# Tile shapes on TensorE: a full-height low key part, transposes in a queue with the value matmuls, and sample scores side by side

## The chip, the cores and the metric

The kernel runs on one core of a Trainium2 chip. The metric is the device time of one execution, in microseconds (us). The engines are TensorE (PE, its weight loads shown apart as PEld), VectorE (DVE), ScalarE (ACT), GpSimd (POOL) and SyncE (SP), which issues most of the loads and stores.

## The reference

Shortened. One layer of a hybrid decoder, for a prompt of 512 tokens and for 8 samples of 4 tokens each that have a past of 2048 positions in a paged cache. The width is 1024.

```python
h = rmsnorm(x, w['g_mix'])
(q, kc_new, vc_new, ks_new, vs_new, kw_new, vw_new, g_nsa, xm, vm, om, i_pre, f_pre) = split_cols(h @ w['w_in'])
...
k_cmp = compress(kc_all, *w['cmp_k'])
v_cmp = compress(vc_all, *w['cmp_v'])
...
o_nsa = nsa_attend(q, k_cmp, v_cmp, ks_all, vs_all, kw_all, vw_all, gates, offset, w_pre)
...
hm, C, n, m = mlstm_chunked(qm, km, vm, i_pre + w['b_i'], f_pre + w['b_f'], C0, n0, m0)
...
x = x + jnp.concatenate([o_nsa, hm], axis=-1) @ w['w_out']
x = x + CrossAttn(rmsnorm(x, w['g_xa']), mem_k, mem_v)
h = rmsnorm(x, w['g_ffn'])
x = x + (jax.nn.silu(h @ w['w_gate']) * (h @ w['w_up'])) @ w['w_down']
y = rmsnorm(x, w['g_final'])
```

`nsa_attend` has 8 query heads over 2 key/value heads of width 64 and sums three softmax branches with gates: compressed blocks, the 16 best blocks of 64 keys, and a window of 512. For the prompt the selected and the windowed branch are plain causal attention over the up to 512 keys before a query; `br` below counts these two. All is float32, and a position's bias is its distance times a slope of the head.

## The kernel before

The 512 prompt tokens and the 32 sample tokens stand together as T = 544 columns, in two halves of 272. A dense matmul in float32 is made of three (`mm3`, L214 to L216): both operands are split into a high and a low part, and high by high, high by low and low by high are summed in one PSUM bank (`bd`, `xa`, `xc`).

A unit of prompt attention is (j, i, br): j of 4 heads in a group, i of 4 blocks of 128 queries, br of 2 branches, 32 units in all, and in each unit v runs over the two key/value heads. A unit goes through three steps:

- `score` (L566 to L591). For each v, L580 multiplies the 128 rows of Q2 (its high part in 64 rows and its low part in the other 64) by KK (the high part of the keys, standing twice, in both halves of the rows), and L581 adds the 64 rows with the high part of the queries times KL, the low part of the keys, which stands only in the rows of its own v. So L580 uses all 128 rows of the array and L581 uses 64. Then DVE adds the bias and finds the extreme (L585), ACT takes the exponential with a sum (L587), DVE the reciprocal (L588), and POOL scales by it and by the gate (L589).
- `turned` (L593 to L601). PE transposes the i + 1 blocks of 128 keys of each v by a matmul with the identity (L599, into one of two `tp` banks), and ACT copies them to SBUF (L601).
- `value` (L603 to L614). For each key block and v, L609 multiplies by 64 columns of values, so that it fills 64 of the array's 128 columns; v = 0 and v = 1 stand in different columns.

The generator (L616 to L625) emits the score of unit n, then the values of unit n - 2, then the transposes of unit n - 1. `weave` (L288) mixes it with the dense matmuls of the projections that follow; when those are used up, the rest of prompt attention is drained alone. The Tile framework then sets the final order on each engine, so matmuls that are emitted together may be taken apart; `tc.issue_after(x)` makes what is emitted inside it, on the same engine, stand behind x.

Sample attention (`sample`, L1375 to L1664) works on two groups g of four samples. Keys come from window buffers and by indirect loads that POOL issues (`gather`, L536), are transposed by PE in fours (`four_t`, L1474) and copied into one of four buffers `kt` (`keys`). The scores of a chunk of 512 keys are four matmuls, one for each sample of the group, each on 32 of the array's columns:

```python
for q, b in enumerate(bs):
    nc.tensor.matmul(S[32 * q:32 * q + 32], Qn[:, b], kts[q], start=True, stop=True)
```

This form stands at L1512 (window), at L1553 (compressed keys, 127 of them) and at L1604 (selected keys, four chunks for each group). Behind it DVE adds a mask and finds the extreme (L1605). The values follow at L1645 in the same 32-column form. This stage is woven with the second part of the compression.

Two more places: mLSTM's gate (L771) multiplies `nsel` by `M2`, 36 rows high; and at the end `to_rows` (L2466 to L2501) transposes the output tiles back to rows, of which the last has only the 32 sample tokens.

Of the kernel before, what the change touches and what calls it, by code (L numbers as in the profile page):

```python
# [16 lines left out]
T = 544  # L17
# [3 lines left out]
EPS = 1e-6  # L21
# [15 lines left out]
def body(tc, I, O, stage=99, dbg=None):  # L37
    nc = tc.nc
    with ExitStack() as top:
# [335 lines left out]
        KL = nn.tile([128, 2, 512], R32, name="KL")  # L375
        bd = nn.tile([128, 512], F32, name="bd")

        def prep_k():
# [8 lines left out]
            for br in range(2):  # L387
                c0 = 256 + 256 * br
                p = bank(ptp)
                for i in range(4):  # L390
                    nc.tensor.transpose(p[:, 128 * i:128 * i + 128], kvn[:, i, c0:c0 + 128], ident)
                for v in range(2):
                    a, b = slice(64 * v, 64 * v + 64), slice(64 - 64 * v, 128 - 64 * v)
                    nc.scalar.activation(KK[a, br, v], p[a], AF.Copy)
                    nc.vector.tensor_tensor(KL[a, br], p[a], KK[a, br, v], op=OP.subtract)
                    nc.gpsimd.tensor_copy(KK[b, br, v], KK[a, br, v])
                p = bank(ptp)
                nc.tensor.transpose(p[:, :32], kvs[:, c0:c0 + 128], ident[:32, :32])
                nc.vector.tensor_copy(kTs[:, br], p[:, :32])
                yield 2  # L400
# [165 lines left out]
        def nsa():  # L566
# [3 lines left out]
            def score(j, i, br):  # L570
# [5 lines left out]
                for v in range(2):  # L576
                    h = 4 * v + j
                    a = slice(64 * v, 64 * v + 64)
                    S = bank((psp, ppo)[v])
                    nc.tensor.matmul(S[:, :n], Q2[:, h, 128 * i:128 * i + 128], KK[:, br, v, :n], start=True, stop=False)  # L580
                    nc.tensor.matmul(S[:, :n], Q2[a, h, 128 * i:128 * i + 128], KL[a, br, :n], start=False, stop=True)  # L581
# [11 lines left out]
            def turned(j, i, br):  # L593
                n = 128 * i + 128
                for v in range(2):
                    sb = soft.pop((j, i, br, v))
                    p = bank(ptp)
                    for k in range(i + 1):
                        nc.tensor.transpose(p[:, 128 * k:128 * k + 128], sb[:, 128 * k:128 * k + 128], ident)  # L599
                    PT[j, i, br, v] = wp.tile([128, 512], F32, name="PT", bufs=4)  # L600
                    nc.scalar.activation(PT[j, i, br, v][:, :n], p[:, :n], AF.Copy)  # L601
# [123 lines left out]
        def mlstm():  # L725
# [5 lines left out]
            nsel = mq.tile([36, 4, 128], R32, name="nsel")  # L731
            M2 = mq.tile([36, 512], R32, name="M2")
# [11 lines left out]
            nc.vector.tensor_copy(nsel, zer[:36, 0:4, None].to_broadcast([36, 4, 128]))  # L744
            nc.vector.tensor_copy(M2, zer[:36, 0:1].to_broadcast([36, 512]))
# [628 lines left out]
        def sample():  # L1374
# [114 lines left out]
            for g in range(2):  # L1489
# [21 lines left out]
                for q, b in enumerate(bs):  # L1511
                    nc.tensor.matmul(S[32 * q:32 * q + 32], Qn[:, b], kts[q], start=True, stop=True)  # L1512
# [32 lines left out]
            for g in range(2):  # L1545
# [6 lines left out]
                for q, b in enumerate(bs):  # L1552
                    nc.tensor.matmul(pc[32 * q:32 * q + 32, 0:127], Qn[:, b], kcT[:, b, 0:127], start=True, stop=True)  # L1553
# [47 lines left out]
                for c in range(4):  # L1601
                    S = bank(psp)
                    for q, b in enumerate(bs):
                        nc.tensor.matmul(S[32 * q:32 * q + 32], Qn[:, b], kts[q], start=True, stop=True)  # L1604
# [860 lines left out]
        def to_rows(j, hf, p):  # L2465
# [10 lines left out]
            for q, i in enumerate(tiles):  # L2476
                m = tok[i][1]
                if i > 1:
                    nc.vector.tensor_tensor(yt[i][:m, cj], pt_[:m, 128 * q:128 * q + 128], yc[:m, 1, cj], op=OP.mult)
# [4 lines left out]
            for q, i in enumerate(tiles):  # L2484
                t0, m = tok[i]
                nc.tensor.matmul(pr[:m, q:q + 1], acct[:, t0:t0 + m], ones_d[:, 0:1], start=True, stop=True)
            r = rn[:, c0:c0 + n]
            if hf == 1:
                nc.vector.memset(r, 1.0)
            for q0, q1, m in (((0, 3, 128),) if hf == 0 else ((0, 1, 128), (1, 2, 32))):  # L2490
                nc.vector.tensor_scalar(r[:m, q0:q1], pr[:m, q0:q1], EPS, None, op0=OP.add)
            nc.gpsimd.tensor_tensor(r, r, mhalf[:, :n], op=OP.pow)
            for q, i in enumerate(tiles):
                t0, m = tok[i]
                y = yt[i]
                if q == 1:
                    nc.scalar.activation(y[:m], y[:m], AF.Copy, scale=r[:m, 1:2])
                else:
                    nc.vector.tensor_scalar(y[:m], y[:m], r[:m, q:q + 1], None, op0=OP.mult)
                dst = O[Y_P][0, t0:t0 + m] if t0 < 512 else O[Y_S].rearrange("b t d -> (b t) d")  # L2500
                nc.sync.dma_start(dst, y[:m])  # L2501
# [31 lines left out]
```

## Time and profile before

| what | us |
|---|---|
| median of three runs | 1302.64 |
| lowest, highest of them | 1298.22, 1302.9 |
| the profiled execution | 1297.18 |
| its span (first to last instruction) | 1295.2 |

The profile is that of one execution. In it a record's length holds its way through the array, and records overlap, so what a matmul costs PE is the time from its start to the start of the next. The stages, by the trace: projections to 110 us, prompt attention to 277.6, mLSTM and the first compression to 490.8, sample attention to 655.6, output mix and cross attention to 909, the gated feed-forward part to 1259, and the end.

### The profile page before, as it was taken

How to read it: one execution, taken by the hardware profiler on the slowest of the kernel's cores; microseconds unless marked ns; L12 is line 12 of the kernel's file. 1: busy time of each engine (PE TensorE's matmuls, PEld its weight loads, DVE VectorE, ACT ScalarE, POOL GpSimd, SP SyncE). 2: the span in 40 equal slices, each digit the busy share in tenths (PEclk: the TensorE clock that was granted, in tenths of full speed). 3: DMA queues.
4: the chain of work that ended last, by engine and by line, in shares of the span. 5: the costliest groups of instructions: out<-in, count | busy, mean ns of one | idle time of the engine just before them, and what ended most of it. 6: DMA issues, size and time to landing. Idle time of an engine off the chain costs nothing.

```text
span 1295.2 us, 25054 instructions
## 1 busy us (share of the span) xinstructions
PE 1231.2 (95%) x9388; PEld 1087.6 (84%) x9388; DVE 869.1 (67%) x1951; ACT 643.3 (50%) x1494; POOL 580.0 (45%) x692
## 2 busy tenths in 40 slices
PE   7999999999999789999999998999989999999996
PEld 5998777748987577766689988679979999999996
DVE  6246464366978978666665485743898888877874
ACT  4234545475646644456554333432555465465452
POOL 1003233257756765553334110014687377387443
PEclk8998999989999889999999999999989999999998
DMA  6424131023125353455678459942022332332311
GB/s 199 122 51 99 44 136 50 1 67 124 48 83 172 112 201 124 148 174 173 213 198 164 130 152 255 303 152 66 2 66 76 121 99 86 116 101 91 129 51 70
DMA packets 141772, 154.34 MB, mean 119 GB/s; under 512 B 17449, under 2 KB 123689, under 8 KB 141394
## 3 DMA queue, kind: packets, MB, share of 16 engines
q1 hardware_dynamic: 131922, 119.17, 30.8%
q0 software_dynamic: 9728, 33.56, 7.9%
q8 instruction: 74, 1.21, 0.4%
q14 instruction: 48, 0.39, 0.1%
HBM read 141.67 MB, written 13.12 MB: 120 GB/s over the span
## 4 chain that ended last, share of the span: by engine, by line
PE 71%; DVE 12%; DMA 5%; issue 4%; POOL 3%; ACT 2%; SPq 1%; POOLq 0%; DVEq 0%; ACTq 0%
PE xa L2208 7%; PE xc L2208 7%; PE bd L214 6%; PE bd L216 6%; PE bd L215 6%; PE bd L2208 5%; PE tp L2208 5%; PE xa L214 2%; PE tp L599 2%; PE xa L216 2%; PE xa L215 2%; PE sp L1604 1%; PE xc L215 1%; PE xc L214 1%; PE xc L216 1%
## 5 line engine op out<-in xcount | busy, mean ns | idle before, releaser
L210 POOL TENSOR_TENSOR al<-fraw,ah 128x512 fp32r<-128x512 f32 (+1 forms) x104 | 127.2, 1224 | 153.4 <-ACT ah L209 124.8
L209 ACT ACTIVATE whi<-wraw 128x1024 fp32r<-128x1024 f32 (+3 forms) x78 | 67.0, 900 | 64.2 <-DMA wraw<-in_w_xv 28.7
L210 DVE TENSOR_TENSOR wlo<-wraw,whi 128x1024 fp32r<-128x1024 f32 (+3 forms) x78 | 79.5, 1046 | 28.7 <-ACT whi L209 28.5
L209 ACT ACTIVATE ah<-fraw 128x512 fp32r<-128x512 f32 (+1 forms) x112 | 66.0, 594 | 41.5 <-PE xc L2208 11.8
L216 PE MATMUL bd<-w1h,xl 128*128 128x256 f32 x256 | 78.4, 307 | 5.1 <-DVE xl L210 2.9
L589 POOL TENSOR_SCALAR sb<-sb,rs,gat 128x128 f32<-128x128 f32 (+3 forms) x64 | 43.2, 678 | 86.8 <-DVE rs L588 73.3
L214 PE MATMUL bd<-w1h,xh 128*128 128x256 f32 x256 | 78.4, 306 | 0.3 <-ACT xh L209 0.3
L215 PE MATMUL bd<-w1l,xh 128*128 128x256 f32 x256 | 76.0, 297 | 0.0
L216 PEld LDWEIGHTS bd<-w1h,xl 128*128 128x128 f32 x256 | 52.2, 204 | 11.5 <-DVE xl L210 3.7
L214 PEld LDWEIGHTS bd<-w1h,xh 128*128 128x128 f32 x256 | 52.2, 204 | 7.6 <-issue 4.3
L209 ACT ACTIVATE xh<-xf 128x512 fp32r<-128x512 f32 x64 | 40.0, 629 | 33.3 <-DVE xf L1149 13.1
L1152 POOL TENSOR_TENSOR sf<-xf 128x256 f32<-128x256 f32 x48 | 35.5, 740 | 46.9 <-DVE sl L210 38.7
L209 ACT ACTIVATE ah<-sp 128x512 fp32r<-128x512 f32 (+1 forms) x64 | 35.6, 557 | 40.8 <-DVE sp L2148 19.2
L214 PE MATMUL bd<-hhi,whi 128*128 128x272 f32 x176 | 54.1, 308 | 0.2 <-ACT whi L209 0.2
L1149 DVE STREAM_TRANSPOSE xf<-cgat 128x512 f32<-128x512 f32 x64 | 44.9, 702 | 13.8 <-POOL sf L1152 13.4
L215 PE MATMUL bd<-hlo,whi 128*128 128x272 f32 x176 | 53.5, 304 | 0.0
L215 PEld LDWEIGHTS bd<-w1l,xh 128*128 128x128 f32 x256 | 52.2, 204 | 1.0 <-issue 0.7
L216 PE MATMUL bd<-hhi,wlo 128*128 128x272 f32 x176 | 53.0, 301 | 0.0
L601 ACT ACTIVATE PT<-tp 128x128 f32<-128x128 f32 (+3 forms) x64 | 27.7, 436 | 50.7 <-PE tp L599 50.2
L209 ACT ACTIVATE ah<-po 128x512 fp32r<-128x512 f32 (+1 forms) x64 | 35.7, 558 | 29.0 <-PE xa L2208 21.6
L585 DVE CUSTOM_DVE_ANT_0 sb<-po,BM 128x128 f32<-128x128 f32 (+3 forms) x32 | 15.7, 491 | 48.6 <-PE po L581 27.2
L216 PE MATMUL bd<-hh,wlo 128*128 128x272 f32 x160 | 46.9, 293 | 0.0
(997 smaller groups left out, 4985.7 us busy)
## 6 DMA issues: line engine op xcount, KB each, us to landing
fraw<-in_w_gate SPq DMA_DIRECT2D x11, 1024.0 KB
fraw<-in_w_up SPq DMA_DIRECT2D x11, 1024.0 KB
fraw<-in_w_down SPq DMA_DIRECT2D x24, 384.0 KB
mkv<-in_cache_mem_k SPq DMA_DIRECT2D x64, 128.0 KB
mkv<-in_cache_mem_v SPq DMA_DIRECT2D x16, 512.0 KB
wraw<-in_w_in SPq DMA_DIRECT2D x8, 512.0 KB
wraw<-in_w_xq SPq DMA_DIRECT2D x4, 1024.0 KB
wraw<-in_w_xk SPq DMA_DIRECT2D x4, 1024.0 KB
```

The source lines that it names most:

```text
L209: nc.scalar.activation(hi, src, AF.Copy)
L210: (eng or nc.gpsimd).tensor_tensor(lo, src, hi, op=OP.subtract)
L214: nc.tensor.matmul(out, ah, bh, start=first, stop=False, **kw)
L215: nc.tensor.matmul(out, ah, bl, start=False, stop=False, **kw)
L216: nc.tensor.matmul(out, al, bh, start=False, stop=last, **kw)
L585: nc.vector.tensor_tensor_reduce(sb[:, :n], S[:, :n], BM[v][:, 384 - 128 * i:512], 1.0, BIG, op0=OP.add, op1=OP.min, accum_out=mn)
L589: (nc.vector, nc.gpsimd)[1].tensor_scalar(sb[:, :n], sb[:, :n], rs, gat[:, i, 3 * h + 1 + br:3 * h + 2 + br], op0=OP.mult, op1=OP.mult)
L599: nc.tensor.transpose(p[:, 128 * k:128 * k + 128], sb[:, 128 * k:128 * k + 128], ident)
L601: nc.scalar.activation(PT[j, i, br, v][:, :n], p[:, :n], AF.Copy)
L1149: nc.vector.transpose(xf.rearrange("p a (q i) -> p q a i", q=4), gs[0].rearrange("p (q t a i) -> p t q a i", q=4, t=4, a=4)[:, t])
L1152: (nc.gpsimd if (1,1,1,1,1,0,1,0)[4 * kv + t] else nc.vector).tensor_tensor(sf, xf[:, :, 0:128:2], xf[:, :, 1:128:2], op=OP.add)
L2208: nc.tensor.matmul(p[:, :HALF], w[a][:, k], x[b_][:, k], start=first and k == 0 and i == 0, stop=last and k == n - 1 and i == 2, skip_grou ...
```

## The change

- KL is kept apart for each v and in full height: four more copies on POOL put it into the other 64 rows too, and L581 multiplies all 128 rows. The product gains the queries' low part times the keys' low part.
- `turned` takes one v. The transposes of v = 1 come first, and the value matmuls of unit n - 2 and the transposes of v = 0 are queued behind them on PE.
- `nsel` and `M2` get 68 rows instead of 36, the new ones zero.
- `quad` issues the four score matmuls of a chunk of sample keys, the fourth sample's first and the other three queued behind it. It is used at the three places named above.
- `to_rows` transposes 128 tokens for the last tile too (those from T - 128 on), whose sample tokens then stand in the partitions 96 to 127; its sums of squares likewise, and one `tensor_scalar` takes the place of a `memset` and two.

```diff
--- before.py
+++ after.py
@@ -372,7 +372,7 @@
-        KL = nn.tile([128, 2, 512], R32, name="KL")
+        KL = nn.tile([128, 2, 2, 512], R32, name="KL")
...
                     nc.scalar.activation(KK[a, br, v], p[a], AF.Copy)
-                    nc.vector.tensor_tensor(KL[a, br], p[a], KK[a, br, v], op=OP.subtract)
+                    nc.vector.tensor_tensor(KL[a, br, v], p[a], KK[a, br, v], op=OP.subtract)
                     nc.gpsimd.tensor_copy(KK[b, br, v], KK[a, br, v])
+                    nc.gpsimd.tensor_copy(KL[b, br, v], KL[a, br, v])
...
@@ -575,10 +576,9 @@
-                    a = slice(64 * v, 64 * v + 64)
                     S = bank((psp, ppo)[v])
                     nc.tensor.matmul(S[:, :n], Q2[:, h, 128 * i:128 * i + 128], KK[:, br, v, :n], start=True, stop=False)
-                    nc.tensor.matmul(S[:, :n], Q2[a, h, 128 * i:128 * i + 128], KL[a, br, :n], start=False, stop=True)
+                    nc.tensor.matmul(S[:, :n], Q2[:, h, 128 * i:128 * i + 128], KL[:, br, v, :n], start=False, stop=True)
...
-            def turned(j, i, br):
+            def turned(j, i, br, v):
                 n = 128 * i + 128
-                for v in range(2):
-                    sb = soft.pop((j, i, br, v))
-                    p = bank(ptp)
-                    for k in range(i + 1):
-                        nc.tensor.transpose(p[:, 128 * k:128 * k + 128], sb[:, 128 * k:128 * k + 128], ident)
-                    PT[j, i, br, v] = wp.tile([128, 512], F32, name="PT", bufs=4)
-                    nc.scalar.activation(PT[j, i, br, v][:, :n], p[:, :n], AF.Copy)
+                sb = soft.pop((j, i, br, v))
+                p = bank(ptp)
+                for k in range(i + 1):
+                    ins = nc.tensor.transpose(p[:, 128 * k:128 * k + 128], sb[:, 128 * k:128 * k + 128], ident)
+                PT[j, i, br, v] = wp.tile([128, 512], F32, name="PT", bufs=4)
+                nc.scalar.activation(PT[j, i, br, v][:, :n], p[:, :n], AF.Copy)
+                return ins.ins
...
-                if n >= 2:
+                if 1 <= n <= len(units):
+                    with tc.issue_after(turned(*units[n - 1], 1)):
+                        if n >= 2:
+                            value(*units[n - 2])
+                        turned(*units[n - 1], 0)
+                elif n >= 2:
                     value(*units[n - 2])
-                if 1 <= n <= len(units):
-                    turned(*units[n - 1])
                 yield
...
@@ -728,8 +731,8 @@
-            nsel = mq.tile([36, 4, 128], R32, name="nsel")
-            M2 = mq.tile([36, 512], R32, name="M2")
+            nsel = mq.tile([68, 4, 128], R32, name="nsel")
+            M2 = mq.tile([68, 512], R32, name="M2")
...
@@ -1479,6 +1482,14 @@
+            def quad(S, bs, keys_of):
+                def one(q):
+                    return nc.tensor.matmul(S[32 * q:32 * q + 32], Qn[:, bs[q]], keys_of(q), start=True, stop=True)
+
+                with tc.issue_after(one(3).ins):
+                    for q in range(3):
+                        one(q)
+
...
@@ -1600,8 +1609,7 @@
-                    for q, b in enumerate(bs):
-                        nc.tensor.matmul(S[32 * q:32 * q + 32], Qn[:, b], kts[q], start=True, stop=True)
+                    quad(S, bs, lambda q: kts[q])
...
@@ -2468,37 +2476,35 @@
             for q, i in enumerate(tiles):
-                t0, m = tok[i]
-                nc.tensor.transpose(pt_[:m, 128 * q:128 * q + 128], xT[:, j, t0:t0 + m], ident)
+                t0 = min(128 * i, T - 128)
+                nc.tensor.transpose(pt_[:, 128 * q:128 * q + 128], xT[:, j, t0:t0 + 128], ident)
...
-            if hf == 1:
-                nc.vector.memset(r, 1.0)
-            for q0, q1, m in (((0, 3, 128),) if hf == 0 else ((0, 1, 128), (1, 2, 32))):
-                nc.vector.tensor_scalar(r[:m, q0:q1], pr[:m, q0:q1], EPS, None, op0=OP.add)
+            nc.vector.tensor_scalar(r, pr[:, :n], EPS, None, op0=OP.add)
```

The order of PE in prompt attention, about j = 0, i = 3: `sp` and `po` are the scores of v = 0 and v = 1, `tp` the transposes, and the values `xa<-PT,kvn` are given with their 64 output columns. Before:

```order
L216 MATMUL bd<-hhi,wlo 128x272
L609 MATMUL xa<-PT,kvn 64x128 x5
L599 MATMUL tp<-ident,sb 128x128 x3
L580 MATMUL po<-KK,Q_107 128x512
L581 MATMUL po<-KL,Q_107 128x512
L609 MATMUL xa<-PT,kvn 64x128
L599 MATMUL tp<-ident,sb 128x128 x2
L580 MATMUL sp<-KK,Q_107 128x128
L599 MATMUL tp<-ident,sb 128x128
L581 MATMUL sp<-KL,Q_107 128x128
L599 MATMUL tp<-ident,sb 128x128
```

The same place on PE after the change:

```order
L216 MATMUL bd<-hhi,wlo 128x272
L580 MATMUL sp<-KK,Q_107 128x512
L581 MATMUL sp<-KL,Q_107 128x512
L598 MATMUL tp<-ident,sb 128x128 x3
L609 MATMUL xa<-PT,kvn 64x128 x6
L598 MATMUL tp<-ident,sb 128x128 x3
L580 MATMUL po<-KK,Q_107 128x512
L581 MATMUL po<-KL,Q_107 128x512
L214 MATMUL bd<-hhi,whi 128x272
```

The six value matmuls of a unit stand together, between the transposes of the two heads, and no longer apart. Over the whole stage the values stand in 64 groups on PE before and in 35 after, with the same number of matmuls; the 64 matmuls of L581 stay where they were, each behind its L580.

The order of PE in sample attention, group g = 1, where the selected keys are scored (`sp<-kt,Qn`) between transposes of gathered keys (`tp<-ident,gat`) and the last of the compression (`xc<-`). Before:

```order
L1177 MATMUL xc<-ident,ys 128x128 x4
L1474 MATMUL tp<-ident,gat 128x128 x20
L1604 MATMUL sp<-kt,Qn 32x512 x4
L1207 MATMUL xc<-w_5548,hid 127x64 x4
L1474 MATMUL tp<-ident,gat 128x128 x4
L1604 MATMUL sp<-kt,Qn 32x512
L1474 MATMUL tp<-ident,gat 128x128 x4
L1604 MATMUL sp<-kt,Qn 32x512 x2
L1474 MATMUL tp<-ident,gat 128x128 x4
L1604 MATMUL sp<-kt,Qn 32x512
L1474 MATMUL tp<-ident,gat 128x128 x8
L1604 MATMUL sp<-kt,Qn 32x512
```

After:

```order
L1477 MATMUL tp<-ident,gat 128x128 x4
L1210 MATMUL xc<-w_5552,hid 127x64 x4
L1477 MATMUL tp<-ident,gat 128x128 x8
L1180 MATMUL xc<-ident,ys 128x128 x4
L1477 MATMUL tp<-ident,gat 128x128 x12
L1487 MATMUL sp<-kt,Qn 32x512 x4
L1477 MATMUL tp<-ident,gat 128x128 x8
L1210 MATMUL xc<-w_5552,hid 127x64 x4
L1477 MATMUL tp<-ident,gat 128x128 x4
L1487 MATMUL sp<-kt,Qn 32x512 x4
L1477 MATMUL tp<-ident,gat 128x128 x12
```

The scores of a chunk stand together, behind the transposes of all four samples. In the whole stage PE's order has 32 places with score matmuls before (30 of them over 512 keys) and 12 after (10 over 512 keys), with the same number of matmuls; the value matmuls L1645 stand at 27 places before and at 23 after.

## Rows read from the trace of the kernel before

**Rows 1.** The profile page of the kernel before, its first part: busy time of each engine, its share of the span, and its instructions.

```profile
PE 1231.2 (95%) x9388; PEld 1087.6 (84%) x9388; DVE 869.1 (67%) x1951; ACT 643.3 (50%) x1494; POOL 580.0 (45%) x692
```

**Rows 2.** Busy time of each engine in two stretches of the span (prompt attention, sample attention), and at the last line from the end of the mLSTM stage to the start of sample attention. Columns: the stretch, its length, then busy us (and instructions) of PE, PEld, DVE, ACT and POOL, the granted TensorE clock, the busy share of the DMA engines, GB/s.

```profile
110.00:277.60 167.60, 166.60 (x1108) 127.11 (x1106) 81.70 (x291) 89.00 (x252) 56.80 (x92) 0.98 0.24 72
...
490.80:655.60 164.80, 161.20 (x1330) 117.92 (x1329) 108.84 (x264) 92.48 (x194) 72.40 (x78) 1.00 0.53 169
...
440.00:496.00 56.00, 43.62 (x287) 39.29 (x286) 46.41 (x115) 25.31 (x61) 34.82 (x44) 0.85 0.52 176
```

**Rows 3.** The chain of work that ended last inside three stretches, as shares of the stretch by engine, tile and line: prompt attention (110 to 277.6), the first part of sample attention (490.8 to 600), and its last part (600 to 655.6). The view breaks its lines off at the end.

```profile
by line: PE tp L599 16.3%; PE bd L214 13.9%; PE bd L216 13.3%; PE bd L215 13.2%; PE xa L609 10.1%; PE xc L609 10.1%; PE sp L581 6.0%; PE po L581 6.0%; PE po L580 3.4%; PE sp L580 2.9%; DMA wraw<-in_w_in 2.6%; SPq L182 1.3%; POOL cgat L536 0
...
by line: PE tp L1474 12.7%; PE sp L1604 10.7%; PE bd L214 9.3%; PE bd L216 8.8%; PE bd L215 8.2%; PE sp L1512 6.2%; PE xa L214 5.7%; PE po L1645 5.1%; PE xc L1207 4.9%; PE xa L216 4.6%; PE xa L215 4.3%; PE sp L1355 3.7%; PE xc L1177 2.4%; P
...
by line: issue 33.8%; PE sp L1604 12.5%; DMA wraw<-in_w_out 7.2%; PE tp L1474 5.5%; ACT SS L1624 3.8%; POOL M L1593 3.6%; POOL gat L536 2.9%; DVE wlo L210 2.7%; POOL xl L210 2.3%; PE xc L214 2.2%; ACT whi L209 2.0%; PE xc L216 1.9%; PE xa L
```

**Rows 4.** The timeline of PE at two scores of prompt attention, one over 512 and one over 256 keys. Columns: start, length of the record, engine, line, tiles, rows*columns of the array that are used, shape. What an instruction costs the engine is read from start to start.

```profile
182.32 0.40 PE L580 MATMUL sp<-KK,Q 128*128 128x512 f32 x1
182.64 0.50 PE L581 MATMUL sp<-KL,Q 64*128 64x512 f32 x1
183.07 0.39 PE L214 MATMUL bd<-hhi,whi 128*128 128x272 f32 x1
183.30 0.29 PE L215 MATMUL bd<-hlo,whi 128*128 128x272 f32 x1
183.43 0.29 PE L216 MATMUL bd<-hhi,wlo 128*128 128x272 f32 x1
...
160.17 0.36 PE L580 MATMUL sp<-KK,Q 128*128 128x256 f32 x1
...
161.00 0.29 PE L216 MATMUL bd<-hhi,wlo 128*128 128x272 f32 x1
```

**Rows 5.** All records of line 581 (the low part of the scores): count, length in ns (least, median, most), first and last start, shapes.

```profile
L581 PE MATMUL sp<-KL,Q x32: 322/409/502, 110.3 to 267.7; 64*128 64x128 f32 x8, 64*128 64x256 f32 x8, 64*128 64x384 f32 x8, 64*128 64x512 f32 x8
L581 PE MATMUL po<-KL,Q x32: 323/409/502, 110.8 to 268.5; 64*128 64x128 f32 x8, 64*128 64x256 f32 x8, 64*128 64x384 f32 x8, 64*128 64x512 f32 x8
```

**Rows 6.** The timeline of PE at two places with value matmuls (two records for each of the program's matmuls), columns as in rows 4.

```profile
184.02 0.65 PE L609 MATMUL xc<-PT,kvn 128*64 128x128 f32 x6
184.60 0.55 PE L599 MATMUL tp<-ident,sb 128*128 128x128 f32 x3
...
186.32 0.43 PE L609 MATMUL xc<-PT,kvn 128*64 128x128 f32 x2
186.68 0.55 PE L599 MATMUL tp<-ident,sb 128*128 128x128 f32 x3
```

**Rows 7.** The four steps of prompt attention's softmax at 512 keys and one of the three dense lines, from the groups by shape in 110 to 277.6: count, then busy us and mean ns of one, then idle time before them and its releasers; and from the waits of the same stretch the one of weight loads on the scale (total us, times, longest).

```profile
L585 DVE CUSTOM_DVE_ANT_0 sb<-sp,BM 128x512 f32<-128x512 f32 x8 | 5.5, 690 | 3.9 <-PE sp L581 2.4 <-POOL sb L589 0.9 <-PE tp L599 0.6
...
L587 ACT ACTIVATE sb<-sb,mn 128x512 f32<-128x512 f32 x16 | 11.5, 717 | 3.1 <-DVE mn L585 3.1
...
L588 DVE RECIPROCAL rs<-rs 128x1 f32<-128x1 f32 x64 | 9.8, 159 | 13.6 <-ACT sb L587 13.5
...
L589 POOL TENSOR_SCALAR sb<-sb,rs,gat 128x512 f32<-128x512 f32 x16 | 13.5, 845 | 23.0 <-DVE rs L588 18.4 <-DVE xc L644 2.5 <-PE tp L599 2.0
...
L214 PE MATMUL bd<-hhi,whi 128*128 128x272 f32 x161 | 49.8, 309 | 0.2 <-ACT whi L209 0.2
...
PEld tp L599 <- POOL sb L589: 2.0, 6, 1.1
```

**Rows 8.** The timeline of PE at a lone score matmul of sample attention and at four that stand together (two records for each of the program's matmuls), columns as in rows 4.

```profile
609.04 0.66 PE L1474 MATMUL tp<-ident,gat 128*128 128x128 f32 x4
609.62 1.04 PE L1604 MATMUL sp<-kt,Qn 128*32 128x512 f32 x2
610.60 0.39 PE L216 MATMUL bd<-w1h,xl 128*128 128x256 f32 x1
610.83 0.28 PE L214 MATMUL bd<-w1h,xh 128*128 128x256 f32 x1
...
552.82 1.06 PE L1604 MATMUL sp<-kt,Qn 128*32 128x512 f32 x8
553.82 1.10 PE L1207 MATMUL xc<-w,hid 128*127 128x64 f32 x8
```

**Rows 9.** All records of the sample scores: L1604 and L1512 over 512 keys. Columns as in rows 5.

```profile
L1604 PE MATMUL sp<-kt,Qn x64: 592/605/617, 535.8 to 639.7; 128*32 128x512 f32 x64
...
L1512 PE MATMUL sp<-kt,Qn x16: 592/605/617, 496.0 to 523.5; 128*32 128x512 f32 x16
```

**Rows 10.** From the waits in 490 to 660: total us, times, longest; and the longest pieces of the chain in 600 to 655.6 (start, us, what).

```profile
POOL gat L536 <- PE tp L1474: 21.3, 8, 14.3
...
604.22 14.11 issue
...
642.54 2.13 ACT SS L1624 x6
```

**Rows 11.** All records of three more lines: the mLSTM gate, the copies of the high key part on POOL, and the transposes at the end; columns as in rows 5.

```profile
L771 PE MATMUL po<-M,nsel x4: 492/492/792, 277.9 to 315.1; 36*128 36x512 f32 x4
...
L396 POOL CAST KK<-KK x4: 605/610/612, 72.7 to 78.7; 64x512 fp32r<-64x512 f32 x4
...
L2472 PE MATMUL tp<-ident,oF x40: 270/272/328, 1259.7 to 1283.4; 128*128 128x128 f32 x32, 128*32 128x128 f32 x8
```

More of the change, by code (lines that the diff above doesn't have):

```diff
@@ L743, in mlstm @@
             load_qk(1)
-            nc.vector.tensor_copy(nsel, zer[:36, 0:4, None].to_broadcast([36, 4, 128]))
-            nc.vector.tensor_copy(M2, zer[:36, 0:1].to_broadcast([36, 512]))
+            nc.vector.tensor_copy(nsel, zer[:68, 0:4, None].to_broadcast([68, 4, 128]))
+            nc.vector.tensor_copy(M2, zer[:68, 0:1].to_broadcast([68, 512]))
             for r in (0, 32):
@@ L1551, in sample @@
                 pc = bank(psp)
-                for q, b in enumerate(bs):
-                    nc.tensor.matmul(pc[32 * q:32 * q + 32, 0:127], Qn[:, b], kcT[:, b, 0:127], start=True, stop=True)
+                quad(pc[:, 0:127], bs, lambda q: kcT[:, bs[q], 0:127])
                 pcs = sc.tile([128, 128], F32, name="pcs")
@@ L1602, in sample @@
                     S = bank(psp)
-                    for q, b in enumerate(bs):
-                        nc.tensor.matmul(S[32 * q:32 * q + 32], Qn[:, b], kts[q], start=True, stop=True)
+                    quad(S, bs, lambda q: kts[q])
                     nc.vector.tensor_tensor_reduce(SS[:, 512 * c:512 * c + 512], S, M4.rearrange("p i c -> p (i c)"), 1.0, BIG, op0=OP.add, op1=OP.min,
@@ L2476, in to_rows @@
             for q, i in enumerate(tiles):
-                m = tok[i][1]
+                m = slice(128 - tok[i][1], 128)
                 if i > 1:
-                    nc.vector.tensor_tensor(yt[i][:m, cj], pt_[:m, 128 * q:128 * q + 128], yc[:m, 1, cj], op=OP.mult)
+                    nc.vector.tensor_tensor(yt[i][m, cj], pt_[m, 128 * q:128 * q + 128], yc[m, 1, cj], op=OP.mult)
             if j < 7:
@@ L2484, in to_rows @@
             for q, i in enumerate(tiles):
-                t0, m = tok[i]
-                nc.tensor.matmul(pr[:m, q:q + 1], acct[:, t0:t0 + m], ones_d[:, 0:1], start=True, stop=True)
+                t0 = min(128 * i, T - 128)
+                nc.tensor.matmul(pr[:, q:q + 1], acct[:, t0:t0 + 128], ones_d[:, 0:1], start=True, stop=True)
             r = rn[:, c0:c0 + n]
-            if hf == 1:
-                nc.vector.memset(r, 1.0)
-            for q0, q1, m in (((0, 3, 128),) if hf == 0 else ((0, 1, 128), (1, 2, 32))):
-                nc.vector.tensor_scalar(r[:m, q0:q1], pr[:m, q0:q1], EPS, None, op0=OP.add)
+            nc.vector.tensor_scalar(r, pr[:, :n], EPS, None, op0=OP.add)
             nc.gpsimd.tensor_tensor(r, r, mhalf[:, :n], op=OP.pow)
@@ L2494, in to_rows @@
                 t0, m = tok[i]
-                y = yt[i]
+                m_ = slice(128 - m, 128)
+                y = yt[i][m_]
                 if q == 1:
-                    nc.scalar.activation(y[:m], y[:m], AF.Copy, scale=r[:m, 1:2])
+                    nc.scalar.activation(y, y, AF.Copy, scale=r[m_, 1:2])
                 else:
-                    nc.vector.tensor_scalar(y[:m], y[:m], r[:m, q:q + 1], None, op0=OP.mult)
+                    nc.vector.tensor_scalar(y, y, r[m_, q:q + 1], None, op0=OP.mult)
                 dst = O[Y_P][0, t0:t0 + m] if t0 < 512 else O[Y_S].rearrange("b t d -> (b t) d")
-                nc.sync.dma_start(dst, y[:m])
+                nc.sync.dma_start(dst, y)
         ws = [take() for _ in range(8)]
```

## The prediction

> **What bounds the kernel now.** I read the engines' busy shares first: PE is busy 95% of the span, the next engine, DVE, 67% [rows 1]. Whether that is one engine's bound everywhere is read by stage. In prompt attention PE is busy 166.60 of 167.60 us, DVE 81.70, ACT 89.00, POOL 56.80; in sample attention PE is busy 161.20 of 164.80, DVE 108.84, ACT 92.48 [rows 2]. The chains agree for prompt attention and for sample attention up to 600 us: nearly every share is a PE line. From 600 on they do not: a third of that chain is "issue", and POOL, ACT and a weight load stand in it [rows 3], with one piece of 14.11 us of issue from 604.22 on [rows 10]. So a microsecond less of PE work is worth about one in the first two stretches, and little between 604 and 618.
>
> Busy PE is not PE at work, though. In the timeline, dense matmuls of 272 columns follow each other in 0.13 us (183.30 to 183.43). L580 over 512 columns, at the same rate 0.125 x 512 / 272 = 0.235, takes 0.32 until L581 starts; L581 takes 0.43 until the next one starts, and that one, a plain dense matmul, 0.23 [rows 4]. L581 uses 64*128 of the array and its neighbours 128*128: each time the shape changes, something is paid on both sides.
>
> **L581 in full height.** From L580's start to the second dense start is 0.98 us (182.32 to 183.30); at the plain rate it is 0.235 + 0.235 + 0.125 = 0.595, so the visit costs 0.385 too much. Over 256 columns it is 0.83 (160.17 to 161.00) against 0.12 + 0.12 + 0.125 = 0.365, so 0.465 [rows 4]. There are 64 such visits [rows 5]. Ends: 64 x 0.30 = 19 (if narrow visits or those beside other odd shapes pay less) and 64 x 0.465 = 30. I take 0.40, 25.6, less 2 for the sides on which a value block stands, which keeps its own switch: 23.5 us of PE. The shape over 128 rows streams the same columns, so nothing is added. The four more POOL copies are priced by their twins, 0.61 us each at 72.7 to 78.7 us [rows 11]; the first score is at 110.3 [rows 5], so 31 us of slack hide them; without that cover they cost 2.4.
>
> The Trainium skill, "TensorEngine Tiling (Array Packing)", Theoretical Speedup and When to Use Tiling, speaks against this edit: a contraction of 64 rows may run as two row tiles at up to twice the speed, which full height gives up. It would hold only where two such matmuls lie side by side, and in these rows each stands alone between full-height ones; the same page's Key Properties say that a change of tiling mode drains the engine, and the 0.23 us of the plain matmul behind L581 agrees. By the first rule the sum would lose some 5 us of the 23.5.
>
> **Values and transposes in a queue.** L609 uses 64 of the columns. One alone takes 0.36 us to the next start (186.32 to 186.68); three together 0.58 (184.02 to 184.60) [rows 6], so a further one costs 0.11 and a visit 0.25; with the slowed instruction before or after it up to 0.35. PE's order has 64 groups of them before and 35 after: 29 x 0.3 = 8.7 us (ends 7 and 10). In prompt attention together 32 us, ends 26 and 40.
>
> What is late next there: the softmax. For 512 keys one head takes 0.69 on DVE, 0.72 on ACT, 0.16, and 0.85 on POOL, 2.4 us [rows 7], and the transposes of v = 1 wait for the last of it. Queued behind them on PE now are the values of unit n - 2 and the transposes of v = 0, and behind those ACT's copy of PT. So far weight loads of transposes waited for the scale six times, 2.0 us in all [rows 7]. A unit takes 167.6 / 32 = 5.2 us now and would take 4.2. The dense matmuls between units run out some three units earlier, and there a unit has nothing that covers these 2.4 us; I charge 1.2 us for each, 4 in all: 32 becomes 28. ACT's 89.00 and DVE's 81.70 stay far under 140.
>
> **Sample scores side by side.** A lone score matmul over 512 keys takes 0.98 us (609.62 to 610.60); four together take 1.00 (552.82 to 553.82). Entry and exit: four transposes take 0.58 before it (609.04 to 609.62), where four at the 0.11 of [rows 6] are 0.44, and the dense matmul behind it 0.23 instead of 0.12 [rows 8]. A visit is 0.98 + 0.14 + 0.11 = 1.23, with one matmul or four. There are 80 matmuls [rows 9] at 30 places of PE's order before and 10 after: 20 x 1.23 = 24.6 us of PE; those over 127 keys stand together already.
>
> How much reaches the end is less plain than in prompt attention. The 7 places of L1512 (all before 524 us [rows 9]) and the 12 of L1604 for group 0 become 6, so 13 of the 20 visits that go lie before 600 us, where the chain is PE: 16 us. The 11 places for group 1, the first at 609.62 [rows 8], become 4. But PE runs close to gathers, evacuations and DVE there (108.84 of 164.80 [rows 2]), and a score now waits for all four copies, so the fourth sample's stands at PE's head with whatever is queued behind it, and the four `kt` buffers come free together. I take three quarters, 12. Of these seven, three lie in the piece that the issue of gathers covers, 604 to 618 [rows 10], and count nothing; the last four (4.9 us) run on the chain until it goes over to ACT at 642.54 [rows 10], and count 3. Together 15, ends 0 and 25.
>
> **mLSTM and the end.** Four gate matmuls over 36 rows [rows 11] become 68 rows high, which uses the whole array's height: 4 x 0.3 = 1.2, of which I count 1. At the end 8 of 40 transposes are 32 columns wide [rows 11]; at 0.14 for a switch that is 1.1, of which I count 1, with the two small DVE instructions that go.
>
> Sum: 28 + 15 + 1 + 1 = 45 us. The profiled execution took 1297.18; less 45 is 1252.2. The median shown is 5.5 above that execution, so 1257.6 beside it: 1258.
>
> **Rivals.**
>
> 1. *All of PE's gain reaches the end.* Nothing waits, as PE's 166.60 of 167.60 and its 161.20 of 164.80 suggest [rows 2]: 32 + 24.6 + 2 = 59 off, or 1244. Against it: the chain after 600 [rows 3]. Chance 0.18.
> 2. *Sample attention turns to its other bounds.* PE's saving is waited off: for gathers (POOL waits 21.3 us for transposes to free their buffers [rows 10], and its loads then land later than PE wants them), for the four `kt` copies, for DVE. There is a second price: where PE waits, the granted clock falls, 0.85 in 440 to 496, where PE is busy 43.62 of 56 [rows 2], a stretch of the lower level (1.2 GHz) in part. Then only prompt attention and the small edits count: 1302.6 - 30 = 1273. Chance 0.20. The Trainium skill, "TensorEngine Tiling (Array Packing)", PSUM Bottleneck, states this as a rule: tiles side by side speed up TensorE and not the copies out of PSUM, which may then bound. By [rows 2] the stage's DVE and ACT shares agree with it only in part, being two thirds of PE's.
> 3. *The change doesn't do what it says in prompt attention:* the cost around L581 comes from its operands (a second weight load from the same rows), not from the shape. Then 64 visits stay, the values' 8.7 and the sample's 15 remain: 1302.6 - 26 = 1277. Against it: the dense matmul behind is slowed as well, and so are the neighbours of L609 and L1604, which have other operands [rows 4, 8]. Chance 0.06.
> 4. *Slower: the head of PE's queue.* The transposes of v = 1 wait for POOL's scale while ready values stand behind them. If what is exposed reaches 32 / 32 = 1.0 us a unit, prompt attention gains nothing; from (28 + 17 + 4) / 32 = 1.5 us a unit the whole kernel is slower. The chain of 2.4 us a head, two heads one after the other on DVE, is long enough. At 1.9 us a unit, 61 us, it comes to 1302.6 + 12 = 1315. Against it: the next unit's scores and some 1.9 us of dense matmuls a unit (161 of each of the three dense lines at 0.125 over 32 units) stand between, and now six waits sum to 2.0 us [rows 7]. Chance 0.04.
>
> **How the numbers follow.** Forecast 0.50, rivals 0.18, 0.20, 0.06, 0.04, and 0.02 for the second and third at once, which leaves the values' 8.7 and 2. The forecast's own range is 1249 to 1267. The range for 8 in 10 reaches from the first rival with the upper ends of the prices (1302.6 - 40 - 25 - 2 = 1236) past the second and third to 1279. A measurement of this kernel can tell about 0.5%, 6.5 us, from no change. Faster by more: the forecast, the first two rivals and most of the third, 0.93. Within it: the rest of the third and the case of both, 0.03. Slower: the fourth, 0.04.
>
> **What would show it.** Right: the matmul behind L581 at 0.125 us and L580 to L581 at 0.235; prompt attention near 140 us with PE still busy throughout; ten visits of 512-key scores at 1.0 us each, and sample attention near 150. Wrong: transposes of v = 1 that wait for POOL beyond 1 us in most units; PE idle in sample attention behind `kt` copies or gathers; a granted clock under 0.95 there; an interval around L581 that stays at 0.98 us.

## The result, and the profile after

The changed kernel takes 1266.54 us (median of four runs, 1264.55 to 1271.56) against 1302.77 before: a ratio of 0.9735, 95% interval 0.9699 to 0.9771, or 36 us less. Forecast were 1258 and 45 us less.

The profiled execution took 1266.96 us, its span 1265.0. First part of the page, as in [rows 1]:

```profile
PE 1186.8 (94%) x9388; PEld 1083.2 (86%) x9388; DVE 869.0 (69%) x1949; ACT 641.4 (51%) x1494; POOL 579.3 (46%) x696
```

PE has the same number of matmuls and is busy 44 us less, but the span fell by only 30.2. Where the rest stayed is seen by stretches. The three below run from the first score of prompt attention to its last value matmul, from there to the first copy of the sample queries, and from there to the last value matmul of sample attention; columns as in [rows 2]. The kernel before:

```profile
110.20:277.60 167.40, 166.40 (x1106) 126.91 (x1105) 81.70 (x291) 89.00 (x252) 56.80 (x92) 0.98 0.24 72
...
277.60:490.90 213.30, 188.82 (x1401) 164.46 (x1400) 175.07 (x399) 122.39 (x335) 149.09 (x170) 0.93 0.36 116
...
490.90:655.70 164.80, 161.20 (x1331) 117.92 (x1330) 108.84 (x264) 92.58 (x194) 72.40 (x78) 1.00 0.53 169
```

The changed kernel:

```profile
109.20:245.20 136.00, 132.91 (x1108) 116.78 (x1106) 81.74 (x291) 87.87 (x252) 57.98 (x92) 0.99 0.29 88
...
245.20:465.70 220.50, 195.33 (x1403) 168.93 (x1402) 172.81 (x400) 122.54 (x337) 145.00 (x170) 0.90 0.36 113
...
465.70:624.70 159.00, 143.77 (x1328) 118.00 (x1327) 106.24 (x263) 92.29 (x193) 72.01 (x78) 0.97 0.54 175
```

Prompt attention is 31.4 us shorter. The stretch behind it, which the change hardly touches, is 7.2 longer, with 6.5 us more of busy PE and a granted clock of 0.90 instead of 0.93. Sample attention is 5.8 shorter, though PE is busy 17.4 us less in it: its idle time went from 3.6 to 15.2 us.

The shape's price is gone where it was to go. The timeline of PE at a score over 512 keys in the changed kernel, as in [rows 4]:

```profile
176.93 0.40 PE L580 MATMUL po<-KK,Q 128*128 128x512 f32 x1
177.16 0.40 PE L581 MATMUL po<-KL,Q 128*128 128x512 f32 x1
177.40 0.29 PE L215 MATMUL bd<-hlo,whi 128*128 128x272 f32 x1
177.52 0.29 PE L216 MATMUL bd<-hhi,wlo 128*128 128x272 f32 x1
```

From L580's start to the second plain matmul 0.59 us, where it was 0.98; each step is at the plain rate. And the head of PE's queue did not become a wait. From the changed kernel's waits in prompt attention (total us, times, longest), as the last line of [rows 7]:

```profile
PEld tp L598 <- POOL sb L589: 2.0, 2, 1.8
...
PE tp L598 <- POOL sb L589: 1.5, 1, 1.5
```

### The profile page after: what moved, and what is told of

It is laid out like the page before. It is cut to its first block, busy times and chain, and to the rows that moved or that the text cites. A ratio compares the mean times of both kernels' runs of the same rounds, so it can differ in the third digit from the quotient of the medians.

```text
span 1265.0 us, 24989 instructions
## 1 busy us (share of the span) xinstructions
PE 1186.8 (94%) x9388; PEld 1083.2 (86%) x9388; DVE 869.0 (69%) x1949; ACT 641.4 (51%) x1494; POOL 579.3 (46%) x696
## 4 chain that ended last, share of the span: by engine, by line
PE 74%; DVE 12%; DMA 5%; ACT 3%; issue 3%; POOL 1%; SPq 1%; another core or an unknown queue 0%; POOLq 0%; DVEq 0%; ACTq 0%
PE xc L2216 7%; PE xa L2216 7%; PE bd L216 6%; PE bd L214 6%; PE bd L215 6%; PE bd L2216 5%; PE tp L2216 5%; PE xa L214 3%; PE xa L216 2%; PE xa L215 2%; PE tp L598 2%; PE xc L215 2%; PE xc L216 2%; PE xc L214 2%; DMA wraw<-in_w_out 2%
## 5 line engine op out<-in xcount | busy, mean ns | idle before, releaser
L209 ACT ACTIVATE ah<-fraw 128x512 fp32r<-128x512 f32 (+1 forms) x112 | 66.0, 594 | 40.2 <-PE xc L2216 11.4
L589 POOL TENSOR_SCALAR sb<-sb,rs,gat 128x128 f32<-128x128 f32 (+3 forms) x64 | 44.4, 697 | 57.2 <-DVE rs L588 46.5
L209 ACT ACTIVATE ah<-sp 128x512 fp32r<-128x512 f32 (+1 forms) x64 | 35.6, 557 | 41.5 <-DVE sp L2156 21.5
L1155 POOL TENSOR_TENSOR sf<-xf 128x256 f32<-128x256 f32 x48 | 34.3, 714 | 43.4 <-DVE sl L210 37.8
L214 PE MATMUL xa<-wsh,sh 128*128 128x256 f32 x128 | 42.1, 329 | 6.8 <-ACT sh L209 6.4
L210 DVE TENSOR_TENSOR al<-sp,ah 128x512 fp32r<-128x512 f32 (+1 forms) x64 | 40.8, 638 | 9.1 <-ACT ah L209 7.4
L1834 POOL TENSOR_TENSOR acc<-acc,sq 128x272 f32<-128x272 f32 x35 | 30.9, 882 | 35.2 <-ACT sq L1833 34.7
```

The lines of the kernel that those rows point to most:

```text
L209: nc.scalar.activation(hi, src, AF.Copy)
L210: (eng or nc.gpsimd).tensor_tensor(lo, src, hi, op=OP.subtract)
L214: nc.tensor.matmul(out, ah, bh, start=first, stop=False, **kw)
L589: (nc.vector, nc.gpsimd)[1].tensor_scalar(sb[:, :n], sb[:, :n], rs, gat[:, i, 3 * h + 1 + br:3 * h + 2 + br], op0=OP.mult, op1=OP.mult)
L1155: (nc.gpsimd if (1,1,1,1,1,0,1,0)[4 * kv + t] else nc.vector).tensor_tensor(sf, xf[:, :, 0:128:2], xf[:, :, 1:128:2], op=OP.add)
L1834: nc.gpsimd.tensor_tensor(acc[hf], acc[hf], sq, op=OP.add)
```

## The experiments

All stretches in one table, in us, each from the one profile of its run; "between" is the stretch from the end of prompt attention to the sample queries. The runs were taken on several chips, and the kernel before, timed beside each, has medians from 1297.86 to 1302.94 us there; so whole times of different runs are compared by their ratios.

| run | ratio to before (95%) | prompt attention | between | sample attention |
|---|---|---|---|---|
| before | | 167.4 | 213.3 | 164.8 |
| before again | | 166.6 | 215.3 | 165.0 |
| small edits alone | 1.0015 (0.9997 to 1.0033) | 167.3 | 213.2 | 166.1 |
| quads alone | 0.9916 (0.9890 to 0.9942) | 166.7 | 216.9 | 153.1 |
| copies, 64 rows | 1.0041 (1.0023 to 1.0060) | 168.2 | 218.5 | 165.9 |
| full-height KL alone | 0.9932 (0.9908 to 0.9956) | 149.5 | 220.9 | 169.2 |
| queue alone | 0.9952 (0.9935 to 0.9969) | 155.4 | 225.4 | 166.9 |
| all but the quads | 0.9788 (0.9761 to 0.9815) | 137.7 | 219.9 | 170.4 |
| changed, 64 rows | 0.9829 (0.9797 to 0.9861) | 155.6 | 218.1 | 148.6 |
| changed | 0.9735 (0.9699 to 0.9771) | 136.0 | 220.5 | 159.0 |
| changed again | | 136.5 | 220.8 | 153.1 |
| changed, other order | 0.9705 (0.9684 to 0.9726) | 137.7 | 219.6 | 154.8 |
| changed, third order | 0.9721 (0.9706 to 0.9736) | 135.9 | 221.8 | 151.0 |
| changed, five kt | 0.9680 (0.9659 to 0.9701) | 137.3 | 218.0 | 142.5 |

### One part at a time

The kernel before with the KL edits alone:

```diff
-                    nc.tensor.matmul(S[:, :n], Q2[a, h, 128 * i:128 * i + 128], KL[a, br, :n], start=False, stop=True)
+                    nc.tensor.matmul(S[:, :n], Q2[:, h, 128 * i:128 * i + 128], KL[:, br, v, :n], start=False, stop=True)
```

> The kernel before with the full-height KL alone. Shape theory (a change of array shape on either side of L581 costs 0.40 us a visit): the interval from L580 to the plain matmul behind falls from 0.98 to about 0.6 at 512 keys, prompt attention gets 23 us shorter, and 17 to 23 us of it reach the end, less what the mLSTM stage gives back. Operand theory (the cost is that of a second weight load from the same rows): the interval stays near 0.98, prompt attention changes by under 3 us, ratio 0.998 to 1.002.

Prompt attention fell by 17.9 us, just under the low end of the price (19) and far from the operand theory's 3. The order changed too; the section on shape against order takes that out. At the end 0.68% arrived, 9 us: the stretch between took 7.6 back and sample attention 4.4.

With `turned` split and the values queued, alone (the edits of `turned` and of the generator in the change):

> The kernel before with the split and queued transposes alone. Shape theory: 29 fewer visits of 64-column value matmuls at 0.3 us, prompt attention 8 to 9 us shorter, the end 6 to 9 us earlier. Head-of-queue theory (the transposes of v = 1 wait for POOL's scale with ready work behind them): prompt attention the same or longer, with waits of PE for L589 well over the 2.8 us of before.

Prompt attention fell by 12.0, more than the 8 to 9 expected, and PE waited for L589 2.7 us (1.8 and 0.9), no more than before. The end moved by 0.48%, 6 us, within what was expected; the stretch between was 12 us longer.

With `quad` alone at its three places:

> The kernel before with the four side-by-side score matmuls alone. If PE bounds sample attention: that stage 15 to 24 us shorter and the kernel with it, ratio 0.981 to 0.988. If the stage goes over to its other bounds (DVE, gathers, key copies): PE's busy time there falls by about 20 us, but the stage by only 0 to 8, ratio 0.994 to 1.0, with new PE waits.

Between the two: sample attention fell by 11.7 us while PE's busy time there fell by 22.7, to 138.51 us. The end moved by 0.84%, 11 us. Part of both falls is work that moved: of the 192 dense matmuls of the output mix on `mh` and `ml`, 96 stood in this stretch before and 53 do here. The other 43 run behind it, and at 0.125 us each they are some 5.4 us (an estimate from the interval of [rows 4]).

```profile
492.50:645.60 153.10, 138.51 (x1295) 113.23 (x1293) 104.78 (x260) 92.03 (x194) 72.07 (x78) 0.97 0.54 175
```

The changed kernel with the loop in place of `quad`:

> The changed kernel with the sample scores in the loop of before. If the quads are worth 15 us or more beside the other edits: about 1281 us. If the changed kernel got under 8 us from them: 1267 to 1274. If the stall of DVE ahead of the first window scores (5.2 us at 473.7 in the changed kernel) comes with the quads, it is absent here and present in the run of the quads alone.

1276.43, between the two, and 10 us above the changed kernel. Sample attention takes 170.4 us without the quads, against 159.0 and 153.1 in the two profiles of the changed kernel and 148.6 with 64 rows, which has the changed kernel's order; the stretch holds the same matmuls in all four. So the quads give 11 to 22 us there, by the execution. Without them, and with 64 rows:

```profile
467.20:637.60 170.40, 162.80 (x1328) 120.31 (x1327) 103.20 (x262) 92.50 (x193) 72.00 (x78) 0.98 0.51 163
```

```profile
484.00:632.60 148.60, 141.35 (x1328) 115.67 (x1327) 106.99 (x263) 91.96 (x193) 71.82 (x78) 0.99 0.58 187
```

The stall of DVE ahead of the first window scores is here too, but shorter (3.7 us of idle DVE), and it is 4.1 us in the run of the quads alone and 5.0 in that of the full-height KL alone, which has no quads; so it does not come with them.

The 68-row gate and the 128-wide last transposes alone:

> The kernel before with the 68-row gate matmuls and the 128-wide last transposes alone. Shape theory: 4 x 0.3 and 8 x 0.14 us, ratio 0.997 to 1.0, the last stretch 0.5 to 1.5 us shorter. If the last stretch is bound by DVE and the stores, no change, 0.999 to 1.001.

Nothing that can be measured; the end from the last dense column on took 50.2 us against 49.9.

### Shape against order

The run of the full-height KL alone also had another order on every engine behind prompt attention. So the same order was run with the old shape: KL kept apart and copied, but multiplied over 64 rows.

```diff
+                    nc.gpsimd.tensor_copy(KL[b, br, v], KL[a, br, v])
...
+                    nc.tensor.matmul(S[:, :n], Q2[64 * v:64 * v + 64, h, 128 * i:128 * i + 128], KL[64 * v:64 * v + 64, br, v, :n], start=False, stop=True)
```

> The kernel before with KL kept apart for each v and the four more POOL copies, while L581 still multiplies 64 rows. Every engine's order is that of the run of the full-height KL alone, word for word; only the shape of L581 differs. Order theory (the full-height edit also moves the order of the mLSTM stage and of sample attention, and this other order is slower by what these stages gave back, 7.6 and 4.4 us): slower than before by 8 to 12 us, ratio 1.006 to 1.009, with some 221 us from the end of prompt attention to the first copy of the sample queries. Fixed-arrival theory (loads or gathers that come at their own time take back what prompt attention gains): the same as before, 0.998 to 1.002, with 211 to 216 us there. By both, the full-height run is 18 to 23 us faster than this one if the shape is what is paid for.

Slower than before by 0.41%, 5 us, though less than expected. The two runs of one order, first with 64 rows, then with 128:

```profile
110.60:278.80 168.20, 166.84 (x1108) 127.12 (x1106) 81.28 (x291) 88.83 (x252) 57.83 (x92) 0.98 0.24 71
```

```profile
108.90:258.40 149.50, 147.87 (x1108) 123.13 (x1106) 81.28 (x291) 87.89 (x252) 58.52 (x92) 0.98 0.26 80
```

18.7 us for 64 visits, all of it busy PE: 0.29 us each. The same was done in the changed kernel:

> The changed kernel with L581 over 64 rows again, in the changed kernel's order word for word. Shape theory: 64 visits at 0.30 to 0.46 us come back, 18 to 25 us, about 1287 us, all of it in prompt attention. Overlap theory (some of that cost is hidden behind the softmax once the values are queued): under 12 us, about 1275.

Prompt attention 155.6 against 136.0: 19.6 us, as the shape theory has it, and nothing hidden. But the whole came to a ratio of 0.9829 against 0.9735, some 12 us above the changed kernel and not 20, since with 64 rows sample attention took 148.6 us in the same order. The first part of that stretch, of the changed kernel and of this one:

```profile
465.70:500.00 34.30, 28.94 (x264) 26.40 (x263) 21.88 (x63) 15.11 (x34) 17.71 (x18) 0.90 0.42 133
```

```profile
484.00:518.30 34.30, 32.55 (x305) 29.45 (x305) 26.66 (x78) 18.92 (x46) 19.14 (x20) 0.95 0.50 162
```

In the same 34.3 us the changed kernel did 41 fewer records on PE, at a lower granted clock. Its timeline shows a hole:

```profile
474.18 1.27 PE L1487 MATMUL sp<-kt,Qn 128*32 128x512 f32 x6
475.04 0.40 PE L1226 MATMUL xc<-w,hid 128*32 128x64 f32 x4
479.70 0.63 PE L1507 MATMUL sp<-kTs,Qn 128*128 128x32 f32 x2 [4.26 <-DVE nmn L1523]
```

DVE waited 5.2 us there for the scores, whose matmuls were over at 475.4 by their records, and PE then for DVE. With 64 rows, in the same order, DVE waited 1.9 us and went on right behind them. Second profiles of both the kernel before and the changed kernel were taken.

> The kernel before once more, for a second profile: what one execution differs from another by, stage by stage. Order theory: the stage from the end of prompt attention to the sample queries is 211 to 217 us again. If it is 219 or more, the 213.3 of the first profile was a lucky execution and there is nothing given back to explain.

215.3, as the order theory has it: the first profile was not a lucky one by more than 2 us.

> The changed kernel once more, for a second profile. If the pause of PE at the first window scores (474 to 479 us, 3.5 us) belongs to this order, it is there again; if it belongs to one execution, it is absent and sample attention is 154 to 157 us instead of 159.0.

Neither as expected: DVE waited there again, 4.1 us instead of 5.2, and PE behind it 2.2 instead of 4.3; but sample attention took 153.1 us, and the execution 1260.94. So the stall comes and goes in size with the execution, and some 6 us of what sample attention seemed to have given back belongs to one execution.

### Does the order decide the stretch between?

```diff
-        burst(fg, 8)
+        burst(fg, 7)
```

> The changed kernel with 7 instead of 8 steps of the mLSTM generator ahead of the first compression, which computes the same; its order from the end of prompt attention to the sample scores is nearer to that of before (PE's rows agree at 0.79 of their places with before, where the changed kernel's agree at 0.49). Order theory (the changed kernel gives back 5 us in this stretch because its order there happened to change): 213 to 217 us from the end of prompt attention to the sample queries, and about 1261 us in all, ratio 0.966 to 0.970. Shorter-attention theory (loads, gathers or DVE work that cannot come earlier take back what prompt attention gained, whatever the order): 219 to 222 us there again, ratio 0.971 to 0.975.

219.6: the order near that of before did not bring the stretch back to 213 to 217. The order theory fails here, as far as a near order can test it; the order of before itself was not run behind a shorter prompt attention.

```diff
-                            (pbd,), cuts=4)), paced(nsg, 1.1))
+                            (pbd,), cuts=4)), paced(nsg, 1.3))
```

> The changed kernel with 1.3 instead of 1.1 as the credit of a step of prompt attention against the dense matmuls; it computes the same, and from the end of prompt attention on PE has the order of the run of the queue alone, which took 225.4 us there. Order theory: 223 to 227 us there, 3 to 7 slower than the changed kernel in that stretch. Shorter-attention theory: 219 to 222 us, as in the changed kernel.

221.8 in an order that took 225.4 in the run of the queue alone. That lies between the two theories, 222 and 223, closer together than two profiles of the kernel before are (2.0 us), so it decides nothing by itself. But in PE's same order, prompt attention is 19.5 us shorter here than in the run of the queue alone and the stretch is 3.6 shorter, not longer; that speaks against the shorter-attention theory. The three orders of the changed kernel cannot be told apart by their whole times: their intervals overlap.

### Buffers behind the quads

```diff
-                kt_ = sc.tile([128, 512], F32, name="kt", bufs=4)
+                kt_ = sc.tile([128, 512], F32, name="kt", bufs=5)
```

> The changed kernel with five instead of four buffers for transposed sample keys. Buffer theory (a quad frees its four buffers together, and the copies of the next chunk wait for it, 3.9 us in the changed kernel): ACT's wait of L202 for the quads falls from 3.9 to under 2 us, PE's idle time in sample attention from 11 to 15 us to 9 or less, 2 to 4 us less in all, ratio 0.969 to 0.972. Other-bounds theory (the idle time is that of gathers, evacuations of transposes and the masks on DVE): PE's idle time stays at 11 to 15 us and the ratio at 0.971 to 0.976.

1254.94 us, ratio 0.9680 (0.9659 to 0.9701): the lowest of all, but its interval meets that of the changed kernel (0.9699 to 0.9771) and overlaps those of the two other orders. Its sample attention, and that of the changed kernel's second profile:

```profile
464.00:606.50 142.50, 135.33 (x1289) 110.62 (x1288) 103.32 (x258) 90.66 (x193) 69.88 (x78) 0.99 0.57 188
```

```profile
467.10:620.20 153.10, 141.90 (x1328) 115.80 (x1327) 106.81 (x262) 91.79 (x193) 72.28 (x78) 0.99 0.56 182
```

PE idles 7.2 us instead of 11.2, and the stretch is 10.6 shorter, more than the 2 to 4 expected. ACT's waits of key copies for the quads, here and in that second profile:

```profile
ACT kt L202 <- PE sp L1487: 2.5, 2, 1.3
```

```profile
ACT kt L202 <- PE sp L1487: 6.4, 3, 2.6
```

They fell, though not under 2. But the 10.6 us are not shown to be the buffer's. As in the run of the quads alone, output-mix matmuls moved: 54 of them stand in this stretch here and 96 in the changed kernel, so 42, an estimated 5.3 us, run behind it. And the pause at the first window scores is absent here (DVE went on 0.09 us behind them), as it is in the run with 64 rows: that one, with four buffers and 6.6 us of the same ACT waits, has PE idle for 7.3 us, against 7.2 here. What the fifth buffer is worth stays open.

## Why the prediction was right, and by how much it missed

**L581 in full height.** The mechanism was right. The term was mis-sized: 23.5 us forecast, 18.7 and 19.6 measured in pairs of one order, 0.29 to 0.31 us a visit. The 0.40 that I took holds where the neighbours are full-height: in the first pair a visit costs 0.39 over 512 and 384 keys and 0.38 over 256, but 0.30 over 128 (0.73 against 0.43 us from L580 to the second plain matmul, three places). The 0.465 that I read over 256 keys was too much, since the plain time there is 0.45 and not 0.365. The 19 visits of that pair that stand beside a value matmul cost 0.14 to 0.28, 3.3 us together, where 0.39 each would be 7.4; I had taken 2 off for these sides, and 4 was due. The operand rival fell: with the same operands twice as high the price was gone. The Trainium skill, "TensorEngine Tiling (Array Packing)", Key Properties, names a drain at each change of tiling mode; the trace agrees that a change costs, 0.39 us for the way into 64 rows and back between full-height matmuls of 256 keys or more.

**The queue.** 8.7 us forecast with ends 7 and 10; measured 12.0 (before), 11.8 (with full height) and 12.6 (with the copies): 0.41 for each of the 29 visits saved, where 0.3 was taken. That the visits are all of it is not shown: the queue also let scores and transposes stand together, which the count of value visits leaves out. Of the 4 us charged for units without cover about half came: PE idled 3.1 of 136.0 us, against 1.0 of 167.4 before. The two misses of price cancelled, by luck: PE's busy time fell by 33.5 us where 32 was forecast, and the stretch by 31.4 where 28 was. The head-of-queue rival found no place.

**The quads.** 24.6 us of PE and 15 at the end were forecast. Over the same matmuls, from 162.80 us of busy PE without them to 143.77, 141.90 and 141.35 with them, they took 19.0 to 21.5 us off PE, so a visit was priced somewhat too high. Off the stage they took 11.4, 17.3 and 21.8 in these three executions, and some 7 to 10 off the whole kernel (ratio 0.9788 to 0.9735, 1276.43 to 1266.54 us). So how much of PE's saving is waited off differs by the execution, from two fifths to nothing, and the "three quarters" lies inside. PE's idle time in the stage is 15.2, 11.2 and 7.3 us; about half of the difference is its wait for DVE behind the first window scores, 4.3, 2.2 and 0.6 us; the sum has no term for it, though the second rival names DVE. The waits of copies for the buffers that a quad holds together are there (3.9, 6.4 and 6.6 us, 1.5 without quads), but the shortest of the three has the longest of them. The second rival holds in part. The Trainium skill, "TensorEngine Tiling (Array Packing)", PSUM Bottleneck, says that copies out of PSUM may bound once tiles run side by side; the trace agrees only in a small part, with 2.9 to 3.4 us in which weight loads of transposes waited for ACT's copies of keys, against 0.8 without the quads.

**What the sum left out.** It took every stretch that the change doesn't touch as unmoved, and sample attention as unmoved but for the quads. The stretch between prompt and sample attention took 7 us back. The KL edits bring another order there, which seven of the profiles share (full-height KL alone, copies with 64 rows, all but the quads, both of the changed kernel, its run with 64 rows and the one with five `kt`): 218.0 to 220.9 us, whether prompt attention took 168 us or 136. The four with the order of before have 213.2 to 216.9. So this other order goes with some 4 us more with prompt attention as long as ever (218.5 with the copies and 64 rows). That an earlier arrival costs more on top is not shown: of the pairs of one order two grew by 2.4 us (218.5 to 220.9, and 218.1 to 220.5), one fell by 3.6, and the profile with five `kt` has 218.0 behind a prompt attention of 137.3. What makes the other order slower is open. PE's idle time in this stretch is alike (24.5 us before, 25.2 after), and its busy time and its granted clock differ, but two profiles of the kernel before differ in these as well (188.82 us at 0.93, 192.58 at 0.90). Sample attention without the quads took 170.4 us and not 164.8, so that of what the quads gave 5.8 remained in the first profile; why is open too.

**mLSTM and the end.** 2 us were counted, none was found.

**From one profile to the median.** The forecast carried the 5.5 us between them over, and that hid part of the miss. From profile to profile the span fell by 30 us, not by 45: prompt attention gave 3.4 more than forecast, the stretch behind it took 7.2, sample attention gave 9.2 less, the small edits 2 less. The medians differ by 36 because the profile of before lies 5.6 us under its median and that of after 0.4 above. So the sum missed by 15 us like for like and by 9 in the medians, and 1266.54 lies at the upper edge of the forecast's own range, 1249 to 1267; that it lies inside is in part luck. The executions of one kernel differ by more than most terms of the sum: 1264.55 to 1271.56 for the changed one.

## What to carry to other kernels

Look on a busy PE for the intervals from start to start around a matmul of another shape than its neighbours: in this kernel, filling the array with rows that add nothing was worth 0.3 us a visit, and gathering odd shapes into blocks 0.4. Before the length of a stage is compared between two kernels, count the matmuls in it: here a stage got some 5 us shorter because work of the next one had moved out of it. When an edit lets a scheduler choose another order, run that order with the edit's effect taken out, before the difference is put down to the edit. And add up a forecast against profiles of both kernels, since one execution can lie 5 us from the median.

## What the runs showed of the hardware

Four score matmuls on 32 columns each, with different operands, take as long as one: 1.00 us against 0.98 [rows 8]. The hole at the first window scores is a second surprise. DVE went on 3.1 to 3.6 us behind the records of the last score matmul in four profiles (with and without quads), 1.2 to 2.1 in four, and under 0.1 in six, among them one with the changed kernel's order word for word; no record explains it. In the four with the longest pause the granted clock then went to its lower level (1.2 GHz) for 3.4 to 10.2 us. In the changed kernel that was from 478.0 to 484.8 us, and the clock is 0.90 over 465.7 to 500 us, where the run of the same order without the hole has 0.95. In that kernel's second profile, where PE waited 2.2 us, no lower level followed. So a pause of PE can cost more than its length.
